# Low part of every second half of a weight tile: an accumulating DMA onto a negated high part in place of a VectorE subtraction

## The chip, the cores and the metric

The kernel runs on one core of one Trainium2 chip. The metric is the device time of one execution in microseconds (us); lower is better. All durations below come from one profiled execution of the kernel before, unless they are called times of runs.

## The reference, cut to what matters

The reference is one decoder block on 256 tokens of width 2048, in float32: an RMS norm, an input projection, two mixers side by side (gated linear attention with four heads, and a gated short convolution), a merge of the two, an output projection with a residual, a second norm, an MLP with a hidden width of 8192, and a last norm.

```python
proj = jnp.einsum('bsd,dn->bsn', h, w_in[l])          # q, k, v, r, lr, cb, cc, cx, ga, gb
...
y_a = jnp.einsum('bse,ed->bsd', o * jax.nn.silu(r), w_gla_out[l])
u = causal_depthwise_conv(cc * cx, conv_w[l])
y_b = jnp.einsum('bsc,cd->bsd', cb * u, w_conv_out[l])
merged = jax.nn.sigmoid(ga) * y_a + jax.nn.sigmoid(gb) * y_b
x = x + jnp.einsum('bsd,de->bse', merged, w_o[l])
hid = jnp.square(jax.nn.relu(jnp.einsum('bsd,df->bsf', h2, w_ffn_up[l])))
x = x + jnp.einsum('bsf,fd->bsd', hid, w_ffn_down[l])
```

Nearly all of the work is matrix products of 256 tokens with large weights: about 300 weight tiles of 1 MB, each read from HBM once.

## The kernel before, in words

**Split products.** Every float32 operand of a large product is split into a high part, rounded to the format float32r, and a low part, the rest. A product is then the sum of three float32r passes: high by high, high by low, low by high. Activations lie in the resident tiles A and B, whose 512 columns hold 256 columns of the high part and 256 of the low part.

**A weight tile.** `wsplit` (L44 to L55) loads one tile of 128 partitions by 2048 columns (1 MB) with a DMA of the SyncE queue into one of 4 buffers `wst` (L45, L46). It then works on two halves of 1024 columns. For each half ScalarE writes the high part `whi` by a rounding copy (L52), and VectorE subtracts it from the loaded half to give the low part `wlo` (L53). `whi` and `wlo` have 5 buffers each, that is two and a half tiles.

**Stationary tiles.** `ws_product` (L57) takes a tile as 16 blocks of 128 columns that are loaded into TensorE as weights. For each block it multiplies `whi` with 512 columns of the activation (L67) and `wlo` with 256 (L69, and L66 for the last block). 221 tiles go this way: the last five of q, those of k, of the convolution branch, of the gates, of the three output projections and of the MLP's up-projection. The first eight blocks use the first half of a tile, the last eight the second. Each product is then gathered by a ScalarE copy (`corr`, L75) and a VectorE addition (L76).

**Moving tiles.** `xs_product` (L408) streams a tile as the moving operand, 24 matmuls of 512 columns per tile (L420 to L422), half of them with the first half of the tile. 78 tiles go this way: those of v and of the MLP's down-projection but two (these two are split at L596 and L597 into the place of B).

**The start.** The first three tiles of q are loaded in quarters into `wst` buffers of their own (L139), split at L165 and L166 while they land, and multiplied at L174 to L176. They take three of the four `wst` buffers. After them TensorE does the small product of the gate's rank-16 input (L185), a sum (L198), and then the first tile that comes by way of `wsplit`.

**Order of the work.** Each engine runs its own list of instructions in order, and waits at each for the buffers and operands that it needs. The list is made when the program is built. A tile's load waits until its `wst` buffer has been read by all four split instructions of the tile that had it before; a split instruction waits until TensorE has finished with the buffer that it overwrites. PSUM holds four product banks (`mmp`).

Of the kernel before, what the change touches and what calls it, by code (L numbers as in the profile page):

```python
# [7 lines left out]
F32 = mybir.dt.float32  # L8
F32R = mybir.dt.float32r
U8 = mybir.dt.uint8  # L10
AF = mybir.ActivationFunctionType
ALU = mybir.AluOpType
PSUM = bass.MemoryType.PSUM

P = 128
T = 256          # tokens
D = 2048
KT = D // P      # contraction tiles of a D-wide product
EPS = 1e-6
# [3 lines left out]
NM = len(LEVELS) * 64 + 128 + 3 * 64  # L23
NQ = 4           # the hidden layer is walked in quarters


@with_exitstack
def block_kernel(ctx, tc, xT, wq, wk, wlr, wv, wr, wcb, wcc, wcx, wga, wgb, wgu,
                 wgla, wconv, wo, wup, wdown, cols, gfin, consts, masks, out):
    """Activations lie transposed ([feature, token]); every float32 operand of a large product is  # L30
    split exactly into two float32r parts and the product is summed from three float32r passes."""
    nc = tc.nc

    cpool = ctx.enter_context(tc.tile_pool(name="cpool", bufs=1))
    apool = ctx.enter_context(tc.tile_pool(name="apool", bufs=1))
    wst = ctx.enter_context(tc.tile_pool(name="wst", bufs=4))
    wsp = ctx.enter_context(tc.tile_pool(name="wsp", bufs=5))
# [4 lines left out]

# [1 line left out]
    def wsplit(src):  # L44
        st = wst.tile([P, 2048], F32, tag="wst", name="wst_t")  # L45
        nc.sync.dma_start(out=st, in_=src)  # L46
        halves = []
        for hf in range(2):
            s = st[:, hf * 1024:(hf + 1) * 1024]
            hi = wsp.tile([P, 1024], F32R, tag="whi", name="whi")  # L50
            lo = wsp.tile([P, 1024], F32R, tag="wlo", name="wlo")
            nc.scalar.copy(out=hi, in_=s)  # L52
            nc.vector.tensor_sub(out=lo, in0=s, in1=hi.bitcast(F32))  # L53
            halves.append((hi, lo))
        return halves  # L55

    def ws_product(src, act):  # L57
        """[128 features, 256 tokens] as (main, correction) in one PSUM bank."""
        halves = wsplit(src)
        ps = mmp.tile([P, 512], F32, tag="mm", name="ps_mm")  # L60
        for kt in range(KT):
            hi, lo = halves[kt // 8]
            sl = slice((kt % 8) * P, (kt % 8 + 1) * P)
            last = kt == KT - 1
            if last:
                nc.tensor.matmul(ps[:, T:], lhsT=lo[:, sl], rhs=act[kt][:, :T], start=False, stop=False)  # L66
            nc.tensor.matmul(ps, lhsT=hi[:, sl], rhs=act[kt], start=(kt == 0), stop=last)  # L67
            if not last:
                nc.tensor.matmul(ps[:, T:], lhsT=lo[:, sl], rhs=act[kt][:, :T], start=False, stop=False)  # L69
        return ps[:, :T], ps[:, T:]  # L70

# [14 lines left out]
    def rsqrt_mean(ms, shape, tag, bufs=1):  # L86
        """1/sqrt(ms) with one Newton step; ms is kept."""
        y = tp.tile(shape, F32, tag=tag, name=tag, bufs=bufs)
        t = tp.tile(shape, F32, tag=tag + "_t", name=tag + "_t", bufs=bufs)
        nc.scalar.activation(t, ms, AF.Sqrt)  # L90
        nc.vector.reciprocal(out=y, in_=t)
        nc.vector.tensor_mul(out=t, in0=y, in1=y)
        nc.vector.scalar_tensor_tensor(out=t, in0=t, scalar=-0.5, in1=ms, op0=ALU.mult, op1=ALU.mult)
        nc.vector.scalar_tensor_tensor(out=y, in0=t, scalar=1.5, in1=y, op0=ALU.add, op1=ALU.mult)
        return y

# [1 line left out]
    A = [apool.tile([P, 512], F32R, tag=f"A{i}", name=f"A{i}") for i in range(KT)]  # L98
# [34 lines left out]

# [1 line left out]
    NF = 3  # L135
    with tc.tile_pool(name="xpool", bufs=1) as xpool:
# [6 lines left out]
        for g in range(4):  # L143
# [14 lines left out]
            for j in range(NF):  # L158
                if g % 2 == 0:
                    fsp[j] = (wsp.tile([P, 1024], F32R, tag="whi", name="whi"),  # L160
                              wsp.tile([P, 1024], F32R, tag="wlo", name="wlo"))
                hi, lo = fsp[j]
                q4 = slice((g % 2) * 512, (g % 2 + 1) * 512)
                ws = fst[j][:, g * 512:(g + 1) * 512]
                nc.scalar.copy(out=hi[:, q4], in_=ws)  # L165
                nc.vector.tensor_sub(out=lo[:, q4], in0=ws, in1=hi[:, q4].bitcast(F32))  # L166
                ps = fps[j]
                for i in range(4):
                    kt = g * 4 + i
                    sl = slice((kt % 8) * P, (kt % 8 + 1) * P)  # L170
                    last = kt == KT - 1
                    if last:
                        nc.tensor.matmul(ps[:, T:], lhsT=lo[:, sl], rhs=A[kt][:, :T], start=False, stop=False)
                    nc.tensor.matmul(ps, lhsT=hi[:, sl], rhs=A[kt], start=(kt == 0), stop=last)  # L174
                    if not last:
                        nc.tensor.matmul(ps[:, T:], lhsT=lo[:, sl], rhs=A[kt][:, :T], start=False, stop=False)  # L176
        nc.sync.dma_start(out=wl_st, in_=wlr)
        nc.sync.dma_start(out=cst, in_=consts)

        # columns 0-15 are the high parts, 32-47 the low ones; the gate product adds their rows  # L180
        nc.scalar.copy(out=wl, in_=wl_st)
# [5 lines left out]
        st = stp.tile([P, T], F32, tag="st", name="st_x")  # L187
        acc = cum[:, 0:2, :]  # cum is not in use yet
        for g in range(8):
# [20 lines left out]

# [1 line left out]
    with tc.tile_pool(name="p2a", bufs=1) as p2a:  # L212
# [5 lines left out]
        def gate(jj):  # L218
            """cum of four tiles: 16 times the log gates, then their sums within each token tile."""
            pgs, abs_ = [], []  # L220
# [37 lines left out]

# [1 line left out]
    def score_level(hd, li):  # L260
# [35 lines left out]
    def score_rest(hd):  # L296
        """The pairs of neighbours: s = t, the levels of one and two tokens; and the keys of the first
        token tile for the queries of the second. Few pairs per query: their products are summed over
        the features by a product with ones, which leaves each sum on every row."""
        hs = slice(2 * hd, 2 * hd + 2)  # L300
# [64 lines left out]
    def next_unit():  # L365
        """The products of the unit prepared a step ago, then the next unit's operands."""
        if ready:
# [8 lines left out]

# [1 line left out]
    pz = [cpool.tile([P, T + 2], F32, name=f"pz{i}") for i in range(2)]  # L378
# [23 lines left out]

# [1 line left out]
    p3 = ExitStack()  # L404
# [3 lines left out]
    def xs_product(srcs, act):  # L408
        """Two PSUM banks [128 tokens, 512] of act^T W."""
        pss = [mmp.tile([P, 512], F32, tag="mm", name="ps_xs") for _ in range(2)]  # L410
# [19 lines left out]

# [1 line left out]
    tb = vp.tile([P, KT, T], F32, name="tb")  # L432
# [43 lines left out]

# [1 line left out]
    o, ssum = o0  # L478
# [18 lines left out]

# [1 line left out]
    sga = vp.tile([P, KT, T], F32, tag="v", name="sga")  # L499
# [9 lines left out]

# [1 line left out]
    mp = ctx.enter_context(tc.tile_pool(name="mp", bufs=1))  # L511
# [27 lines left out]

# [1 line left out]
    ssq = cpool.tile([P, 2, 5], F32, name="ssq")  # L541
# [3 lines left out]
    def down_evac(ps, m, c0, w, k):  # L545
        """Adds a product to the residual; its sum of squares goes to column k of the last norm's."""
        xs = xtok[:, m, c0:c0 + w]
# [36 lines left out]

    # The last chunk's weights stay whole on chip (half of them where the operand B was), so that the
    # first token tile is finished and stored under the products of the second one.
    wres = []
# [30 lines left out]
def _stationary(np, w):  # L618
    """[K, N] -> [N/128, K/2048, 128 (k), 16 (k tile), 128 (n)], one contiguous megabyte per tile."""
    k, n = w.shape  # L620
    return np.ascontiguousarray(
        w.reshape(k // 2048, 16, 128, n // 128, 128).transpose(3, 0, 2, 1, 4)).reshape(-1, 128, 2048)


def _moving(np, w):
    """[K, N] -> [K/2048, N/512, 4, 128 (k), 4 (k tile), 512 (n)], one contiguous megabyte per tile."""
    k, n = w.shape
# [62 lines left out]
```

## Time and profile before

| what | value |
|---|---|
| time of runs before, median of 2 | 1765.72 us (1765.39 to 1766.05) |
| span of the profiled execution, first to last instruction | 1764.1 us |
| what lies outside the span (median less span) | 1.6 us |
| mean granted TensorE clock | 0.999 |
| data read from HBM over the span | 325.17 MB |

The profile gives, for each engine, how long it was busy, what it waited for, and when each instruction ran. PE is TensorE's matmuls, PEld its weight loads, DVE is VectorE, ACT is ScalarE, POOL is GpSimd, SP is SyncE; a q behind the name means the engine's DMA queue. "DMA share" is the mean busy share of the core's 16 DMA engines. A wait is written "who <- whom".

### The profile page before, as it was taken

What the parts mean: (1) busy time and instruction counts of PE and PEld (TensorE: products, weight loads), DVE (VectorE), ACT (ScalarE), POOL (GpSimd) and SP (SyncE); (2) the same over time, 40 slices, a digit from 0 to 9 for tenths busy, and PEclk for the clock granted to TensorE, in tenths of its full rate; (3) what the DMA queues carried; (4) which work ended last, traced back from release to release, by engine and by line L of the source; (5) the groups of instructions that cost most, each with busy time, mean ns of one, the idle gap of its engine ahead of it and who ended that gap; (6) DMA issues with size and microseconds to landing.
All of it is one profiled execution on the core that took longest, in us unless ns stands there. A gap on an engine that the chain in (4) does not pass through costs nothing.

```text
span 1764.1 us, 23853 instructions
## 1 busy us (share of the span) xinstructions
PE 1749.0 (99%) x9468; PEld 1502.3 (85%) x9468; DVE 1161.8 (66%) x1717; ACT 856.3 (49%) x1178; POOL 0.2 (0%) x4
## 2 busy tenths in 40 slices
PE   8999999999999999999999999999999999999998
PEld 6888888888888888888888888888888888888887
DVE  8978888765555558875676666655665566556664
ACT  7745454444344446654544454434443354334451
POOL 0000000000000000000000000000000000000000
PEclk9999999999999999999999999999999999999999
DMA  8454444555555544455555555555555555555552
GB/s 312 169 192 167 167 170 167 177 181 193 196 184 188 191 177 160 166 199 189 191 183 208 213 191 183 187 193 193 188 191 191 191 191 190 192 191 191 181 190 83
DMA packets 50158, 328.81 MB, mean 186 GB/s; under 512 B 5694, under 2 KB 7870, under 8 KB 11391
## 3 DMA queue, kind: packets, MB, share of 16 engines
q1 hardware_dynamic: 47376, 323.55, 51.5%
q10 hardware_dynamic: 2670, 3.74, 0.6%
q8 instruction: 74, 1.21, 0.3%
q14 instruction: 38, 0.30, 0.0%
HBM read 325.17 MB, written 2.10 MB: 186 GB/s over the span
## 4 chain that ended last, share of the span: by engine, by line
PE 99%; DMA 0%; DVE 0%; ACT 0%; SPq 0%; issue 0%; DVEq 0%; ACTq 0%
PE ps_mm L67 47%; PE ps_mm L69 22%; PE ps_xs L421 8%; PE ps_xs L422 8%; PE ps_xs L420 8%; PE ps_mm L66 1%; PE sp L286 1%; PE ps_mm L174 1%; PE ps_xs L612 0%; PE ps_xs L611 0%; PE ps_xs L610 0%; PE po L446 0%; PE ps_mm L176 0%; DMA wst_t<-in_wq 0%; PE ps_lr L185 0%; PE po L448 0%
## 5 line engine op out<-in xcount | busy, mean ns | idle before, releaser
L53 DVE TENSOR_TENSOR wlo<-wst_t,whi 128x1024 fp32r<-128x1024 f32 x598 | 731.5, 1224 | 374.4 <-ACT whi L52 366.1
L52 ACT CAST whi<-wst_t 128x1024 fp32r<-128x1024 f32 x598 | 628.7, 1052 | 483.1 <-PE ps_mm L67 242.0
L67 PE MATMUL ps_mm<-A,whi 128*128 128x512 f32 x2000 | 707.5, 399 | 0.0
L67 PE MATMUL ps_mm<-B,whi 128*128 128x512 f32 x1536 | 538.7, 399 | 0.0
L69 PE MATMUL ps_mm<-A,wlo 128*128 128x256 f32 x1875 | 527.1, 281 | 0.0
L67 PEld LDWEIGHTS ps_mm<-A,whi 128*128 128x128 f32 x2000 | 370.9, 188 | 79.1
L69 PE MATMUL ps_mm<-B,wlo 128*128 128x256 f32 x1440 | 404.5, 281 | 0.0
L69 PEld LDWEIGHTS ps_mm<-A,wlo 128*128 128x128 f32 x1875 | 354.0, 189 | 4.1
L67 PEld LDWEIGHTS ps_mm<-B,whi 128*128 128x128 f32 x1536 | 283.6, 188 | 62.5
L69 PEld LDWEIGHTS ps_mm<-B,wlo 128*128 128x128 f32 x1440 | 271.9, 189 | 4.6
L75 ACT COPY corr<-ps_mm 128x256 f32<-128x256 f32 x208 | 77.3, 372 | 347.0 <-PE ps_mm L67 346.2
L420 PE MATMUL ps_xs<-whi,A 128*128 128x512 f32 x608 | 236.5, 389 | 0.0
L421 PE MATMUL ps_xs<-wlo,A 128*128 128x512 f32 x608 | 236.5, 389 | 0.0
L422 PE MATMUL ps_xs<-whi,A 128*128 128x512 f32 x608 | 236.5, 389 | 0.0
L76 DVE TENSOR_TENSOR t<-ps_mm,corr 128x256 f32<-128x256 f32 x208 | 88.1, 424 | 176.3 <-ACT corr L75 176.1
L421 PEld LDWEIGHTS ps_xs<-wlo,A 128*128 128x128 f32 x608 | 114.1, 188 | 23.8
L420 PEld LDWEIGHTS ps_xs<-whi,A 128*128 128x128 f32 x608 | 114.1, 188 | 23.7
L422 PEld LDWEIGHTS ps_xs<-whi,A 128*128 128x128 f32 x608 | 114.1, 188 | 23.4
L83 ACT CAST A<-t 128x256 fp32r<-128x256 f32 x80 | 32.6, 408 | 7.6 <-DVE t L506 7.4
L66 PE MATMUL ps_mm<-A,wlo 128*128 128x256 f32 x125 | 35.2, 282 | 0.0
L84 DVE TENSOR_TENSOR A<-t,A 128x256 fp32r<-128x256 f32 x80 | 33.5, 419 | 0.0
L548 DVE SCALAR_TENSOR_TENSOR xtok<-ps_xs,rs,xtok 128x512 f32<-128x512 f32 (+1 forms) x33 | 22.8, 728 | 14.5 <-PE ps_xs L612 14.5
(171 smaller groups left out, 798.3 us busy)
## 6 DMA issues: line engine op xcount, KB each, us to landing
wst_t<-in_wup SPq DMA_DIRECT2D x64, 1024.0 KB, 4.8
wst_t<-in_wdown SPq DMA_DIRECT2D x64, 1024.0 KB, 4.8
wst_t<-in_wcc SPq DMA_DIRECT2D x16, 1024.0 KB, 4.8
wst_t<-in_wcx SPq DMA_DIRECT2D x16, 1024.0 KB, 4.8
wst_t<-in_wcb SPq DMA_DIRECT2D x16, 1024.0 KB, 4.8
wst_t<-in_wv SPq DMA_DIRECT2D x16, 1024.0 KB, 4.8
wst_t<-in_wgb SPq DMA_DIRECT2D x16, 1024.0 KB, 4.7
wst_t<-in_wconv SPq DMA_DIRECT2D x16, 1024.0 KB, 4.8
```

The lines of the kernel that those rows point to most:

```text
L52: nc.scalar.copy(out=hi, in_=s)
L53: nc.vector.tensor_sub(out=lo, in0=s, in1=hi.bitcast(F32))
L66: nc.tensor.matmul(ps[:, T:], lhsT=lo[:, sl], rhs=act[kt][:, :T], start=False, stop=False)
L67: nc.tensor.matmul(ps, lhsT=hi[:, sl], rhs=act[kt], start=(kt == 0), stop=last)
L69: nc.tensor.matmul(ps[:, T:], lhsT=lo[:, sl], rhs=act[kt][:, :T], start=False, stop=False)
L75: nc.scalar.copy(out=c, in_=corr)
L76: nc.vector.tensor_add(out=out_t, in0=main, in1=c)
L83: nc.scalar.copy(out=dst[:, :T], in_=src)
L84: nc.vector.tensor_sub(out=dst[:, T:], in0=src, in1=dst[:, :T].bitcast(F32))
L420: nc.tensor.matmul(pss[m], lhsT=ah, rhs=hi[:, sl], start=(kt == 0), stop=False)
L421: nc.tensor.matmul(pss[m], lhsT=ah, rhs=lo[:, sl], start=False, stop=False)
L422: nc.tensor.matmul(pss[m], lhsT=al, rhs=hi[:, sl], start=False, stop=(kt == len(srcs) * 4 - 1))
```

## The change

`wsplit` treats the two halves of a tile differently. The first half is as before. For the second half ScalarE first writes the negated half, rounded, into a tile `wla` (an activation with scale -1), then the high part as before; and a DMA issued by GpSimd adds the same half tile, read a second time from HBM, onto `wla`. Its 1024 columns by 128 partitions are 0.5 MB. VectorE does nothing for the second half. To make room, `wst` goes from 4 buffers to 3 and `wlo` from 5 to 3 (now first halves alone, so three tiles), and `wla` has 4 (four tiles). `whi` keeps its 5. The first three tiles of q still use VectorE alone, with the 3 `wlo` buffers. The rest of the difference is comments.

```diff
-    wst = ctx.enter_context(tc.tile_pool(name="wst", bufs=4))
+    wst = ctx.enter_context(tc.tile_pool(name="wst", bufs=3))
     wsp = ctx.enter_context(tc.tile_pool(name="wsp", bufs=5))
...
     def wsplit(src):
         st = wst.tile([P, 2048], F32, tag="wst", name="wst_t")
         nc.sync.dma_start(out=st, in_=src)
         halves = []
         for hf in range(2):
             s = st[:, hf * 1024:(hf + 1) * 1024]
             hi = wsp.tile([P, 1024], F32R, tag="whi", name="whi")
-            lo = wsp.tile([P, 1024], F32R, tag="wlo", name="wlo")
-            nc.scalar.copy(out=hi, in_=s)
-            nc.vector.tensor_sub(out=lo, in0=s, in1=hi.bitcast(F32))
+            if hf == 0:
+                lo = wsp.tile([P, 1024], F32R, tag="wlo", name="wlo", bufs=3)
+                nc.scalar.copy(out=hi, in_=s)
+                nc.vector.tensor_sub(out=lo, in0=s, in1=hi.bitcast(F32))
+            else:
+                lo = wsp.tile([P, 1024], F32R, tag="wla", name="wla", bufs=4)
+                nc.scalar.activation(lo, s, AF.Copy, scale=-1.0)
+                nc.scalar.copy(out=hi, in_=s)
+                nc.gpsimd.dma_start(out=lo, in_=src[:, 1024:], accum_op=ALU.add)
             halves.append((hi, lo))
         return halves
...
                     fsp[j] = (wsp.tile([P, 1024], F32R, tag="whi", name="whi"),
-                              wsp.tile([P, 1024], F32R, tag="wlo", name="wlo"))
+                              wsp.tile([P, 1024], F32R, tag="wlo", name="wlo", bufs=3))
```

Two places show how the lists of instructions stand. The first is ScalarE's list in the MLP's up-projection, where the numbers behind the names tell the tiles apart: a tile's load is `wst_t_N`, and the next tile's number is higher by 51 or 52. Before, for two products:

```order
L75 COPY corr_9983<-ps_mm_9949 128x256
L52 CAST whi_10094<-wst_t_10092 128x1024
L83 CAST A5_84<-t1_9986 128x256
L52 CAST whi_10098<-wst_t_10092 128x1024
L75 COPY corr_10034<-ps_mm_10000 128x256
L52 CAST whi_10145<-wst_t_10143 128x1024
L83 CAST A6_85<-t1_10037 128x256
L52 CAST whi_10149<-wst_t_10143 128x1024
```

And of the changed kernel, at the same place:

```order
L83 COPY corr_10110<-ps_mm_10076 128x256
L55 CAST whi_10223<-wst_t_10221 128x1024
L91 CAST A4_83<-t1_10113 128x256
L60 CAST whi_10227<-wst_t_10221 128x1024
L59 ACTIVATE wla_10332<-wst_t_10325 128x1024
L83 COPY corr_10162<-ps_mm_10128 128x256
L55 CAST whi_10275<-wst_t_10273 128x1024
L91 CAST A5_84<-t1_10165 128x256
L60 CAST whi_10279<-wst_t_10273 128x1024
L59 ACTIVATE wla_10384<-wst_t_10377 128x1024
```

Between the second high part of a tile (L60) and the gathering of a product (L83 COPY) there now stands the negation (L59) of a tile two further on: 10325 beside 10221.

The second place is GpSimd's list, which before held four fills of constants and nothing of the program's own. Its beginning now, where `wla` is the tile that the DMA adds onto and the name behind the arrow is the weight in HBM:

```order
L690 MEMSET const-uint8-127 128x1
L694 UNCONDITIONAL_BRANCH
L61 DMA wla<-in_wq 128x1024 x5
L61 DMA wla<-in_wk 128x1024 x8
L61 DMA wla<-in_wcc 128x1024
L61 DMA wla<-in_wcx 128x1024
L61 DMA wla<-in_wcb 128x1024
```

There are 299 such DMAs, one for each tile that goes through `wsplit`, in the order of the tiles.

## Rows read from the trace of the kernel before

**Rows 1.** The page, part 1: busy time, share of the span and instructions per engine.

```profile
PE 1749.0 (99%) x9468; PEld 1502.3 (85%) x9468; DVE 1161.8 (66%) x1717; ACT 856.3 (49%) x1178; POOL 0.2 (0%) x4
```

**Rows 2.** The page, part 4: the chain that ended last, shares of the span.

```profile
PE 99%; DMA 0%; DVE 0%; ACT 0%; SPq 0%; issue 0%; DVEq 0%; ACTq 0%
```

**Rows 3.** Timeline of ACT in the up-projection: start, us, engine, line, work [idle <-releaser].

```profile
1064.65 1.05 ACT L52 CAST whi<-wst_t 128x1024 fp32r<-128x1024 f32 x1 [0.97 <-PE ps_mm L67]
1067.61 0.37 ACT L75 COPY corr<-ps_mm 128x256 f32<-128x256 f32 x1 [1.90 <-PE ps_mm L67]
1067.87 1.05 ACT L52 CAST whi<-wst_t 128x1024 fp32r<-128x1024 f32 x1
1068.93 0.41 ACT L83 CAST A<-t 128x256 fp32r<-128x256 f32 x1
1070.30 1.05 ACT L52 CAST whi<-wst_t 128x1024 fp32r<-128x1024 f32 x1 [0.97 <-PE ps_mm L67]
```

**Rows 4.** Timeline of ACT in the down-projection.

```profile
1200.67 1.06 ACT L52 CAST whi<-wst_t 128x1024 fp32r<-128x1024 f32 x1 [1.67 <-PE ps_xs L422]
1203.39 1.05 ACT L52 CAST whi<-wst_t 128x1024 fp32r<-128x1024 f32 x1 [1.66 <-PE ps_xs L422]
1206.12 1.05 ACT L52 CAST whi<-wst_t 128x1024 fp32r<-128x1024 f32 x1 [1.67 <-PE ps_xs L422]
```

**Rows 5.** Groups by line and shape: count, busy us, mean ns, idle before.

```profile
L53 DVE TENSOR_TENSOR wlo<-wst_t,whi 128x1024 fp32r<-128x1024 f32 x598 | 731.5, 1224 | 374.4 <-ACT whi L52 366.1
...
L83 ACT CAST A<-t 128x256 fp32r<-128x256 f32 x80 | 32.6, 408 | 7.6 <-DVE t L506 7.4
...
L270 ACT ACTIVATE e<-e 128x512 f32<-128x512 f32 x20 | 12.6, 629 | 6.5 <-DVE e L268 6.5
...
L155 ACT ACTIVATE A<-xt,colt 128x256 fp32r<-128x256 f32 x16 | 6.9, 498 | 2.4 <-DMA xt<-in_xT 2.4
...
L165 ACT CAST whi<-wst_t 128x512 fp32r<-128x512 f32 x12 | 6.8, 613 | 1.5 <-DMA wst_t<-in_wq 1.5
```

**Rows 6.** Stretches: PE, PEld, DVE, ACT, POOL busy (count), PEclk, DMA share, GB/s.

```profile
40.00:65.00 25.00, 25.00 (x141) 21.80 (x140) 20.89 (x45) 23.32 (x32) 0.00 (x0) 1.00 0.47 170
65.00:90.00 25.00, 25.00 (x144) 21.72 (x143) 25.00 (x50) 13.51 (x21) 0.00 (x0) 1.00 0.52 189
...
10.00:20.00 10.00, 10.00 (x52) 8.45 (x52) 9.88 (x20) 9.72 (x22) 0.00 (x0) 1.00 1.05 403
```

**Rows 7.** DMA from 1200 to 1222 us: queue, packets, MB, share; issues, us to landing.

```profile
q1 hardware_dynamic: 576, 4.19, 54.8%
...
wst_t<-in_wup SPq DMA_DIRECT2D x4, 1024.0 KB, 4.9
```

**Rows 8.** DMA from 30 to 36 us, where the queues of SP (q1) and ACT (q10) overlap.

```profile
q1 hardware_dynamic: 240, 1.74, 74.4%
q10 hardware_dynamic: 113, 0.35, 22.6%
...
wst_t<-in_wk SPq DMA_DIRECT2D x1, 1024.0 KB, 5.3
```

**Rows 9.** DMA from 10 to 20 us, issues: count, KB each, us to landing.

```profile
wst_t<-in_wq SPq DMA_DIRECT2D x1, 1024.0 KB, 7.8
```

**Rows 10.** Timeline of the start: SP's queue, VectorE, TensorE.

```profile
15.31 14.24 SPq L46 DMA_DIRECT2D wst_t<-in_wq  x5
...
21.70 1.90 DVE L166 TENSOR_TENSOR wlo<-wst_t,whi 128x512 fp32r<-128x512 f32 x3
...
30.22 0.58 PE L67 MATMUL ps_mm<-A,whi 128*128 128x512 f32 x1
```

## The prediction, made before the changed kernel ran

> **What bounds the kernel now.** I read the busy times first. TensorE's matmuls cover 1749.0 of the 1764.1 us; VectorE is busy for 66% and ScalarE for 49% [rows 1]. Busy shares alone could deceive, so the chain that ended last came next: 99% of it is TensorE [rows 2]. The 15 us that TensorE is idle lie before its first matmul and behind its last. So what the change takes away, VectorE's work, stands nowhere on the path. Then I looked at what the others wait for, in a timeline of ScalarE: before each rounding copy L52 it sits idle for 0.97 to 1.90 us, released by TensorE [rows 3, 4]. The splitting runs ahead as far as its buffers let it and is held back by TensorE, not the other way round.
>
> The same timelines give the pace. The same copy comes back after 1070.30 - 1064.65 = 5.65 us, the time of a stationary tile [rows 3]; two halves of a moving tile take 1206.12 - 1200.67 = 5.45 us [rows 4]. These are the budgets that every other engine, the DMA engines among them, has to meet. I therefore look for a load that comes to more than 5.45 or 5.65 us per tile.
>
> **VectorE.** 299 subtractions of 1.224 us go [rows 5]: 366 us, which leaves 796 (45%). On the path: 0, as nothing waits for VectorE. Even from 65 to 90 us, where it is busy for 25.00 of 25 us, TensorE is too [rows 6].
>
> **ScalarE.** 299 negations come. The nearest rows: an ACTIVATE is slower than a CAST of the same shape by 16 ns at 512 columns (629 against 613) and by 90 at 256 (498 against 408) [rows 5]; a CAST of 1024 columns takes 1.05 us [rows 3]. So 1.07 to 1.14 us each, I take 1.1: 329 us more, 1185 in all (67%). Per tile of the up-projection: 2 x 1.05 + 0.37 + 0.41 + 1.1 = 4.0 of 5.65 us. Its cover is thus the idle time of ScalarE before L52. It is gone in one place: from 40 to 65 us, with the gates' functions, ScalarE is busy for 23.32 of 25 us [rows 6], and 25 / 5.65 = 4.4 negations add 4.9. That is 3.2 us too many. The split is up to two and a half tiles ahead, some 14 us, and from 65 to 90 us ScalarE has 25 - 13.51 - 4.9 = 6.6 us to catch up. Cost between 0 and 3.2; I take 1.
>
> **The added wait.** ScalarE's negation stands two tiles ahead of the high parts, as the list shows, and waits for that tile's load and for TensorE to end the tile that had its `wla` buffer four tiles before. Behind it stand the gathering copy and the next high parts. Numbering the tile that TensorE has just ended as 1, the negation is that of tile 5 and the next high part that of tile 4. The latter is needed only two tiles later, 11 us, and the sum of `wla` three and a half tiles later, some 19 us. A landing of 4.9 us [rows 7] or 7.8 behind others [rows 9] is hidden by either. With 3 `wst` buffers the load of tile 5 starts when the second high part of tile 2 is done, in the middle of tile 0, and has one and a half tiles, 8.2 us or more, less the copy's 1.05 us. It takes 4.9. What is late next, if transfers get slower, is this load (second rival).
>
> **DMA.** This decides. A full load now takes 54.8% of 22 us for 4.19 MB, or four tiles: 3.0 us of the 16 engines per tile [rows 7]. But these are single transfers with a rise and a fall. Where transfers are queued behind each other the engines moved 403 GB/s at a share of 1.05 [rows 6], so 1.05 MB costs 2.60 us when nothing is left idle. Two queues share the engines: from 30 to 36 us theirs take 74.4% and 22.6% [rows 8], so the shares add up, and a load landed after 5.3 us in place of 4.9.
>
> The accumulating DMA is in no row; nothing in the trace comes from GpSimd's queue. Bounds: its 0.5 MB pass the engines at least once, 1.3 us at the full rate. At most each byte passes three times one after the other, read from HBM, read from SBUF, written: 3.9 us (at the price of single transfers, 4.5). I take 2.6 us, as the nearest row is that of a plain 1 MB load: the accumulation has just as much to read, 0.5 MB from HBM and 0.5 MB of what it adds onto, and a plain copy's writing does not show as a time of its own. Sum per tile: 2.6 + 2.6 = 5.2 us, 92% of 5.65 and 95% of 5.45. It fits, by little. Cost: 0, from 0 to (6.5 - 5.65) x 221 + (6.5 - 5.45) x 78 = 188 + 82 = 270 us.
>
> A rule bears on this. The Trainium skill (Collectives: The Full Stack, The bandwidth ceiling) has it that an add inside the DMA costs nothing of itself, but needs two source reads on the same ring, and gives 62.28 against 32.35 GB/s for a copy and a reduction, a ratio of 1.93. By that the 0.5 MB would be an estimated 1.3 x 1.93 = 2.5 us and the sum 5.1, which fits too; by three passes it would be 6.5, which does not. No run here shows yet which holds.
>
> **GpSimd.** It has 0.2 us of work [rows 1] and now one issue per tile. SyncE's issues are one per tile as well and are never on the chain. I take 0; it would cost only if an issue took more than 5.45 us.
>
> **The start.** Three `wst` buffers are all taken by the first three tiles of q. Before, the fourth tile's load was issued at 15.31 us [rows 10] and landed 7.8 us later [rows 9]. Now it waits for the last subtraction of the first tile, 21.70 us + a third of 1.90, so it is issued at 22.4 and lands after 4.9 to 7.8 us, at 27.3 to 30.2. High part 1.05 and subtraction 1.22: its first half is ready at 29.6 to 32.5, where TensorE wanted it at 30.22 [rows 10]. Its second half: negation until 29.5 to 32.4, then an issue and a landing again like a load's, 34.4 to 40.2, where TensorE wants it at 30.2 + 2.8 = 33.0. So 1.4 to 7 us late; I take 3, nearer to the lower end, as a half tile has half the bytes.
>
> **Sum.** 1764.1 + 1.6 outside the span = 1765.7, which is the median of the runs; + 3 start + 1 gates + 0 = 1770 us. From below: TensorE has no wait to give back, so nothing in the rows can bring more than a few us.
>
> **First rival: the DMA engines become the bound.** It decides as soon as load plus accumulation take over 5.45 (moving) or 5.65 us (stationary), that is from 2.85 or 3.05 us for the accumulation, only 10 to 17% above my value. It costs the excess in every tile. If both transfers cost as in single transfers, 3.0 + 3.0 = 6.0: 0.35 x 221 + 0.55 x 78 = 120 us, so 1886 us. If each byte passes three times, 1765.7 + 270 = 2036 us. For it: the margin of 5 to 8%, the 3.0 us that a load in fact shows, and smaller pieces (rows of 4 KB for 8 KB). Against: the 403 GB/s.
>
> **Second rival: ScalarE held up by a late load.** Load of tile 5, negation of 5, gathering, high parts of 4, which free the buffer for the load of 7: a loop over two tiles. If the load lands after 2.6 + 2.6 + the 2.3 us that 4.9 has beyond its 2.6, because an accumulation always runs beside it, it is 7.5 + 0.3 issue + 1.1 + 0.37 + 0.41 + 2.1 = 11.8 us against 2 x 5.65 = 11.3. That is 0.25 per tile, 55 us over 221: 1821 us. Against it: the accumulation of an earlier tile is issued by the negation that precedes the load's last stretch, so the two overlap only in part.
>
> **Third rival: faster.** TensorE would have to run faster without VectorE's second stream of reads; for 2%, 35 us, a tile would have to take 5.53 in place of 5.65 us: 1730 us. No row supports it: beside a VectorE that is full from 65 to 90 us TensorE is busy throughout at a clock of 1.00 [rows 6].
>
> **How the numbers follow.** Forecast 53%; first rival 34%, second 11%, third 2%. A measurement of this kernel tells about 2% from no change. Both slower rivals lie beyond 1801, so slower has 45%, same 53%, faster 2%. The forecast's own range is 1763 to 1790. For 8 in 10 the range must take in most of the first rival: 1762 to 2036, its three-pass end; what is left out is mainly an accumulation dearer than that.
>
> **What would show it.** Right: a new queue with 157 MB, landing within 10 us; DMA share near 0.9; TensorE still 98% busy; the only new TensorE wait near 30 us. Wrong: TensorE waiting for `wla` in every tile, at L67 or L69 in mid tile, with the DMA share at its ceiling (first rival), or ScalarE's L59 waiting for the load of `wst_t` (second). A tile time above 5.65 us in the up-projection gives the accumulation's price at once.

## The result, and the profile after

The changed kernel takes 1846.18 us (two runs, 1845.93 to 1846.43) against 1765.72 us before: 1.0456 times as long, 95% interval 1.0436 to 1.0475. That is 80.5 us slower. The prediction's likeliest case, 1770 us and no change, did not come; the time lies in the range of 1762 to 2036, and on the side of the slower rivals.

The page of the changed kernel, parts 1, 3 and 4, answers to [rows 1] and [rows 2]:

```profile
PE 1774.9 (96%) x9468; PEld 1503.9 (82%) x9468; DVE 805.3 (44%) x1418; ACT 1111.7 (60%) x1479; POOL 258.4 (14%) x303
...
q0 software_dynamic: 43056, 156.78, 48.7%
q1 hardware_dynamic: 47376, 323.55, 45.9%
...
DMA 45%; PE 26%; ACT 11%; issue 10%; DVE 6%; POOL 0%; ACTq 0%; SPq 0%; DVEq 0%; POOLq 0%
```

VectorE lost the work that it was to lose, 1161.8 to 805.3 us. TensorE's idle time went from 15 to 70 us, and its busy time from 1749 to 1775. A lower clock after stops is a part of these 26 us: the mean granted clock was 0.993 against 0.999, an estimated 0.006 x 1845 = 11 us. But some 15 of the 26 lie in the MLP (633.0 against 618.4 us busy from its first up-projection load to the last), at a mean granted clock of 1.00; that the profile counts short waits of matmuls there as busy time is likely, but not shown. The chain, 99% TensorE before, now runs through DMA for 45%. A quick reading of this page of the profile says: the DMA engines are 95% busy, so they are full. The experiments show that this reading is wrong.

The list of waits of the changed kernel (who <- whom, us in total, times, longest) points elsewhere. Before, none of its long rows had ScalarE waiting for a load:

```profile
ACT wla L59 <- DMA wst_t<-in_wdown: 151.2, 59, 5.3
ACT wla L59 <- DMA wst_t<-in_wup: 151.0, 58, 6.1
...
PE ps_mm L77 <- DVE wlo L56: 15.6, 25, 1.3
...
PE ps_mm L77 <- DMA wla<-in_wq: 8.4, 3, 7.3
```

The negation L59 waits for loads for hundreds of us; this is the sign that the prediction named for its second rival. TensorE waits longest in all for `wlo`, the low part of a *first* half, which no accumulation makes. It is late because its high part stands behind the negation of another tile in ScalarE's list. Only at the start does TensorE wait for an accumulation worth naming.

The timeline of ScalarE, 1250 to 1270 us, shows it (start, us, work, and the idle time before with its releaser); compare [rows 3, 4]:

```profile
1250.50 1.06 ACT L59 ACTIVATE wla<-wst_t 128x1024 fp32r<-128x1024 f32 x1 [1.12 <-DMA wst_t<-in_wdown]
1251.46 1.03 ACT L55 CAST whi<-wst_t 128x1024 fp32r<-128x1024 f32 x1
1252.40 1.05 ACT L60 CAST whi<-wst_t 128x1024 fp32r<-128x1024 f32 x1
1258.58 1.06 ACT L59 ACTIVATE wla<-wst_t 128x1024 fp32r<-128x1024 f32 x1 [5.13 <-DMA wst_t<-in_wup]
1259.54 1.03 ACT L55 CAST whi<-wst_t 128x1024 fp32r<-128x1024 f32 x1
1260.48 1.04 ACT L60 CAST whi<-wst_t 128x1024 fp32r<-128x1024 f32 x1
```

Before, it was TensorE that released the copies. Now ScalarE stands for 5.13 us at a negation whose load has not landed, and then at once does the two high parts of another tile, whose load had landed long before.

The issues of the MLP's loads in the changed kernel, with microseconds to landing (counted from the start of the issue, median), and the time of the first and the last of the 64 up-projection loads. Before, they landed after 4.8:

```profile
wst_t<-in_wup SPq DMA_DIRECT2D x64, 1024.0 KB, 8.0
...
wla<-in_wup POOLq DMA_DIRECT2D x64, 512.0 KB, 8.0
...
L48 SPq DMA_DIRECT2D wst_t<-in_wup x64: 327/328/328, 1060.4 to 1713.7; - x64
```

From the first to the last of them are 111 tiles (63 stationary, 48 moving). They take 653.3 us, 5.89 each; before, the same row ran from 1015.0 to 1633.4, 618.4 us, 5.57 each. So 35 of the 80 us are lost here. This stretch is the yardstick below ("the MLP stretch").

### The profile page after: what moved, and what is told of

Same layout as the page of the kernel before. It is cut to its first block, busy times and chain, and to the rows that moved or that the text cites. A ratio compares the mean times of both kernels' runs of the same rounds, so it can differ in the third digit from the quotient of the medians.

```text
span 1844.6 us, 24535 instructions
## 1 busy us (share of the span) xinstructions
PE 1774.9 (96%) x9468; PEld 1503.9 (82%) x9468; DVE 805.3 (44%) x1418; ACT 1111.7 (60%) x1479; POOL 258.4 (14%) x303
## 3 DMA queue, kind: packets, MB, share of 16 engines
q0 software_dynamic: 43056, 156.78, 48.7%
## 4 chain that ended last, share of the span: by engine, by line
DMA 45%; PE 26%; ACT 11%; issue 10%; DVE 6%; POOL 0%; ACTq 0%; SPq 0%; DVEq 0%; POOLq 0%
PE ps_mm L75 15%; DMA wst_t<-in_wup 12%; DMA wst_t<-in_wdown 11%; PE ps_mm L77 7%; DMA wst_t<-in_wconv 6%; ACT whi L55 5%; DVE wlo L56 4%; DMA wst_t<-in_wga 3%; DMA wst_t<-in_wgla 3%; ACT whi L60 3%; DMA wst_t<-in_wr 3%; DMA wst_t<-in_wv 2%; DMA wst_t<-in_wo 2%; ACT corr L83 1%; ACT wla L59 1%
## 5 line engine op out<-in xcount | busy, mean ns | idle before, releaser
L59 ACT ACTIVATE wla<-wst_t 128x1024 fp32r<-128x1024 f32 x299 | 317.0, 1060 | 623.2 <-DMA wst_t<-in_wdown 151.2
L56 DVE TENSOR_TENSOR wlo<-wst_t,whi 128x1024 fp32r<-128x1024 f32 x299 | 365.8, 1223 | 356.9 <-ACT whi L55 348.9
L60 ACT CAST whi<-wst_t 128x1024 fp32r<-128x1024 f32 x299 | 312.4, 1045 | 10.3 <-PE ps_mm L75 10.3
L77 PE MATMUL ps_mm<-A,wlo 128*128 128x256 f32 x1000 | 283.5, 284 | 6.1 <-DVE wlo L56 6.0
L77 PE MATMUL ps_mm<-A,wla 128*128 128x256 f32 x875 | 247.0, 282 | 8.4 <-DMA wla<-in_wq 8.4
L77 PE MATMUL ps_mm<-B,wlo 128*128 128x256 f32 x768 | 218.5, 285 | 9.8 <-DVE wlo L56 9.6
L77 PEld LDWEIGHTS ps_mm<-A,wlo 128*128 128x128 f32 x1000 | 189.7, 190 | 13.9 <-DVE wlo L56 10.2
L77 PE MATMUL ps_mm<-B,wla 128*128 128x256 f32 x672 | 189.1, 281 | 0.9 <-DMA wla<-in_wup 0.9
L77 PEld LDWEIGHTS ps_mm<-A,wla 128*128 128x128 f32 x875 | 166.4, 190 | 9.4 <-DMA wla<-in_wq 9.4
L77 PEld LDWEIGHTS ps_mm<-B,wlo 128*128 128x128 f32 x768 | 145.8, 190 | 21.8 <-DVE wlo L56 18.1
L429 PE MATMUL ps_xs<-wlo,A 128*128 128x512 f32 x304 | 121.5, 400 | 10.9 <-DVE wlo L56 10.7
L77 PEld LDWEIGHTS ps_mm<-B,wla 128*128 128x128 f32 x672 | 127.2, 189 | 1.3 <-DMA wla<-in_wup 1.3
```

The costliest lines, as they stand in the source:

```text
L59: nc.scalar.activation(lo, s, AF.Copy, scale=-1.0)
L429: nc.tensor.matmul(pss[m], lhsT=ah, rhs=lo[:, sl], start=False, stop=False)
```

## The experiments

Two theories stood against each other. A: the DMA engines are full, a load and an accumulation together take about 5.8 us, more than a tile. B: the engines have room, but ScalarE's list holds up the high parts behind a negation that waits for a load. The loop is: load of tile n, negation of n, the two high parts of n-1, which free the staging buffer (`wst`) for the load of n+2.

**The transfers by themselves.** A kernel of transfers alone, in seven phases:

```diff
+    for i in range(N):                       # accumulating, float32r
+        nc.gpsimd.dma_start(out=d[i % R], in_=w[i, :, 1024:], accum_op=ALU.add)
...
+    for i in range(N):                       # loads of 1 MB beside accumulating ones
+        nc.sync.dma_start(out=fl[i % 3], in_=w[24 + i])
+        nc.gpsimd.dma_start(out=f[i % R], in_=w[i, :, 1024:], accum_op=ALU.add)
```

> Transfers alone, no block computed: seven phases of 24 transfers of 0.5 MB each, four in flight (plain from SyncE; plain from GpSimd; accumulating in float32; accumulating in float32r; accumulating with the source in SBUF; then 24 loads of 1 MB beside 24 accumulations; 24 loads beside 24 plain ones). Theory A (the DMA engines are full, an accumulation costs about twice a plain transfer or more): plain 1.3 us each, accumulating 2.6 to 3.0 us each, a load beside an accumulation together 5.4 to 5.9 us. Theory B (the engines have room, ScalarE's list holds the loads up): accumulating 1.3 to 2.3 us each, load and accumulation together under 5.2 us. If the rounding to float32r costs something, the float32r phase is longer than the float32 one.

The timeline of GpSimd's issues (start, us an issue, and the wait before): plain (`b`), accumulating in float32 (`c`), in float32r (`d`), from SBUF (`e`), beside loads of 1 MB (`f`):

```profile
53.83 0.53 POOL L43 DMA_DIRECT2D b<-in_wup  x1 [0.72 <-DMA b<-in_wup]
55.12 0.53 POOL L43 DMA_DIRECT2D b<-in_wup  x1 [0.76 <-DMA b<-in_wup]
...
101.11 0.86 POOL L47 DMA_DIRECT2D c<-in_wup  x1 [1.66 <-DMA c<-in_wup]
103.58 0.86 POOL L47 DMA_DIRECT2D c<-in_wup  x1 [1.60 <-DMA c<-in_wup]
...
150.85 0.86 POOL L51 DMA_DIRECT2D d<-in_wup  x1 [1.66 <-DMA d<-in_wup]
153.32 0.86 POOL L51 DMA_DIRECT2D d<-in_wup  x1 [1.60 <-DMA d<-in_wup]
...
215.49 0.86 POOL L55 DMA_DIRECT2D e<-a  x1 [1.62 <-DMA e<-a]
217.97 0.85 POOL L55 DMA_DIRECT2D e<-a  x1 [1.62 <-DMA e<-a]
...
318.22 0.86 POOL L62 DMA_DIRECT2D f<-in_wup  x1 [4.16 <-DMA f<-in_wup]
323.22 0.86 POOL L62 DMA_DIRECT2D f<-in_wup  x1 [4.14 <-DMA f<-in_wup]
328.25 0.86 POOL L62 DMA_DIRECT2D f<-in_wup  x1 [4.16 <-DMA f<-in_wup]
```

With four transfers in flight each issue follows a landing, so the distance of two rows is the price: 2.48 us accumulating (217.97 - 215.49), the same in float32, in float32r and from SBUF. Plain, it is 1.3 us where the issues follow each other evenly, as in the two rows; that phase has gaps, with which its mean is 316 GB/s, or 1.66 us a transfer. A pair of a load and an accumulation takes 5.02 us (10.03 over two). That is the capacity: below 5.45 and 5.65. Theory A's price per pair is wrong; the price that theory B gave an accumulation (1.3 to 2.3 us) was a little low.

**Without the accumulation.**

```diff
-                nc.gpsimd.dma_start(out=lo, in_=src[:, 1024:], accum_op=ALU.add)
+                nc.gpsimd.dma_start(out=lo, in_=src[:, 1024:])
```

> The changed kernel with the accumulation left out of the DMA, which copies the half tile plainly; the sum of the low part is therefore left out. Same bytes from HBM, same lists. Theory A: an engine time of about 2.8 + 1.4 = 4.2 us per tile, the waits at L59 vanish but for the start: 1765 to 1785 us. Theory B (the second stream delays the loads, whatever it costs the engines): still 1810 to 1846 us.

1778.06 us, 1.0062 times before (1.0039 to 1.0085). This row speaks for A as it was written down, as plain transfers cost the engines half. It doesn't tell the theories apart after all: loads land after 6.8 us in it, not 8.0, which also takes the loop of theory B off the path (worked out below). The MLP stretch took 618.8 us.

**A fourth staging buffer, and the negation one tile nearer.**

```diff
-    wst = ctx.enter_context(tc.tile_pool(name="wst", bufs=3))
+    wst = ctx.enter_context(tc.tile_pool(name="wst", bufs=4))
...
-                lo = wsp.tile([P, 1024], F32R, tag="wlo", name="wlo", bufs=3)
+                lo = wsp.tile([P, 1024], F32R, tag="wlo", name="wlo", bufs=2)
...
-                lo = wsp.tile([P, 1024], F32R, tag="wla", name="wla", bufs=4)
+                lo = wsp.tile([P, 1024], F32R, tag="wla", name="wla", bufs=3)
...
```

> Four wst buffers again, paid for by one wla (3) and one wlo (2); nothing is left out. The negation is then one tile nearer to its use and its load one tile earlier. Theory A: the tile time stays that of the engines, about 5.8 us; only the start improves: 1820 to 1846 us. Theory B: the loop over load, negation and high part is broken: 1765 to 1785 us.

1778.71 us, 1.0067 (1.0045 to 1.009), with every accumulation in place. Of its page of the profile, part 3, then the list of waits:

```profile
q0 software_dynamic: 43056, 156.78, 49.6%
q1 hardware_dynamic: 47376, 323.55, 47.1%
...
ACT wla L59 <- PE ps_mm L74: 303.0, 201, 1.7
```

The same bytes in the same two queues, at a share of 97%, and in the MLP TensorE is no longer held up: the negation now waits for TensorE. The MLP stretch took 618.3 us (1025.4 to 1643.7), as long as before. Theory A can't stand beside this.

**No negation.** The accumulations go onto four fixed tiles.

```diff
-                lo = wsp.tile([P, 1024], F32R, tag="wla", name="wla", bufs=4)
-                nc.scalar.activation(lo, s, AF.Copy, scale=-1.0)
+                lo = wla4[turn[0] % 4]
+                turn[0] += 1
...
```

> The negation is left out: the DMA accumulates onto four fixed tiles that are zeroed once, so the low parts of second halves are wrong sums. The DMA traffic is that of the changed kernel, ScalarE never waits for a load two tiles ahead. Theory A: the traffic sets the pace: 1825 to 1850 us. Theory B: 1765 to 1785 us.

1781.17 us, 1.008 (1.0051 to 1.0109). With the traffic kept, and the instruction that waits for the load two tiles on taken out of ScalarE's list, the time comes back, though staging has its 3 buffers.

**One number.** The run with four staging buffers changed two things, the staging and the place of the negation; they had to be told apart.

```diff
-                lo = wsp.tile([P, 1024], F32R, tag="wla", name="wla", bufs=4)
+                lo = wsp.tile([P, 1024], F32R, tag="wla", name="wla", bufs=3)
```

> The changed kernel with one number changed: wla has 3 buffers, not 4. The list then has the negation one tile further on instead of two ahead of the next high part; DMA traffic, staging buffers and instruction counts stay. Theory B (ScalarE held up by the load that the negation waits for): the waits of L59 on loads vanish, the tile time returns to 5.65 and 5.45 us, what is left is the start: 1775 to 1785 us. Theory A (engines full at 5.8 us per tile): 1840 to 1850 us. Theory C (the three staging buffers are what is short): still above 1820 us, as loads start no earlier.

1784.08 us, 1.0097 (1.0082 to 1.0112): 62 of the 80 us are back with a buffer *less*. The number of `wla` buffers decides where the negation stands. In the list of the up-projection the negation behind the second high part of a tile is that of the tile two further on with 4 buffers, of the next tile with 3, and of the tile itself with 2. With 3:

```order
L60 CAST whi_10227<-wst_t_10221 128x1024
L59 ACTIVATE wla_10280<-wst_t_10273 128x1024
L83 COPY corr_10162<-ps_mm_10128 128x256
L55 CAST whi_10275<-wst_t_10273 128x1024
```

The negation is that of the very next tile, 10273, whose high part comes two instructions later. ScalarE's timeline, then the row of the whole MLP stretch of this kernel (PE, PEld, DVE, ACT, POOL busy, PEclk, DMA share, GB/s):

```profile
1255.84 1.06 ACT L59 ACTIVATE wla<-wst_t 128x1024 fp32r<-128x1024 f32 x1 [1.61 <-PE ps_mm L74]
1256.80 0.35 ACT L83 COPY corr<-ps_mm 128x256 f32<-128x256 f32 x1
1257.05 1.05 ACT L55 CAST whi<-wst_t 128x1024 fp32r<-128x1024 f32 x1
1258.10 0.41 ACT L91 CAST A<-t 128x256 fp32r<-128x256 f32 x1
1258.83 1.05 ACT L60 CAST whi<-wst_t 128x1024 fp32r<-128x1024 f32 x1 [0.32 <-PE ps_mm L75]
1261.49 1.06 ACT L59 ACTIVATE wla<-wst_t 128x1024 fp32r<-128x1024 f32 x1 [1.61 <-PE ps_mm L74]
...
1069.00:1723.00 654.00, 654.00 (x3329) 555.42 (x3329) 240.45 (x339) 405.62 (x488) 101.97 (x118) 1.00 1.00 284
```

The period is 1261.49 - 1255.84 = 5.65 us again and TensorE has no gap in the stretch. The same stretch of the changed kernel:

```profile
1069.00:1723.00 654.00, 633.73 (x3197) 527.59 (x3196) 226.34 (x324) 372.92 (x463) 95.83 (x111) 1.00 0.97 268
```

With a *higher* DMA share, 1.00 against 0.97, the faster kernel moves 284 against 268 GB/s. Theory C fell too: 3 staging buffers are enough.

**Two buffers for the sums.** The same number, one further down.

```diff
-                lo = wsp.tile([P, 1024], F32R, tag="wla", name="wla", bufs=4)
+                lo = wsp.tile([P, 1024], F32R, tag="wla", name="wla", bufs=2)
```

> The changed kernel with 2 wla buffers. The negation then never waits for a load, but it can run only when TensorE has ended the tile two before: 1.06 us for it, 0.9 for the issue and 7.7 for the landing are 9.7 us, where TensorE gets to the second half after one and a half tiles, 8.5 us. Theory B with this lead time: TensorE waits for wla, some 1.2 us in every tile or, if the waits fall on every second one, half of that: 1850 to 2000 us, and the waits are named wla, not L59 on a load. If only the place of the negation before loads mattered: 1775 to 1790 us, as with 3 buffers.

2189.46 us, 1.24 (1.2275 to 1.2523), far more than expected, with the waits on `wla` that were expected. Of its list of waits:

```profile
PEld ps_xs L429 <- DMA wla<-in_wdown: 103.4, 52, 6.0
...
PE ps_mm L77 <- DMA wla<-in_wup: 71.8, 49, 4.9
```

The mistake was to count the lateness once. It closes on itself: the negation of tile n waits for TensorE to end tile n-2, then come 1.06 us for it, 0.3 until the issue starts, a landing of 10.1 here (the issue is part of it), and half a tile of TensorE, 2.8: 14.3 us for two tiles, 7.1 each. The MLP stretch shows 799.6 / 111 = 7.2. So of the three numbers tried the middle one is best: at 4 the negation meets loads that have not landed, at 2 the sums come too late.

**The start.** Buffers alone, on the kernel before, every low part by VectorE:

```diff
-    wst = ctx.enter_context(tc.tile_pool(name="wst", bufs=4))
+    wst = ctx.enter_context(tc.tile_pool(name="wst", bufs=3))
...
-            lo = wsp.tile([P, 1024], F32R, tag="wlo", name="wlo")
+            lo = wsp.tile([P, 1024], F32R, tag="wlo", name="wlo", bufs=4)
```

> The kernel before with 3 wst buffers and 4 wlo, nothing else: every low part by VectorE, no GpSimd DMA. If the start's loss of some 12 us comes from the fourth tile's load having to wait for a buffer: 1768 to 1775 us. If it comes from the accumulations: 1765 to 1768 us.

1768.85 us, 1.0016 (1.0007 to 1.0026): 3.2 us. And the changed kernel with accumulations from the 14th split tile on:

```diff
+                if turn[0] <= 13:
+                    nc.scalar.copy(out=hi, in_=s)
+                    nc.vector.tensor_sub(out=lo, in0=s, in1=hi.bitcast(F32))
+                else:
```

> The changed kernel, but the 13 tiles of q and k that go through the split get their second low part from VectorE as before (in a wla buffer); accumulations start with the convolution's tiles. If the start and the gates lose 12 to 17 us through ScalarE's and GpSimd's added work there: 1830 to 1838 us; if the buffers alone are the reason, less than 5 us come back: 1841 to 1846 us.

1828.23 us, 18.0 less than the changed kernel, a little more than the 8 to 16 that the first case allowed; the median is below its 1830. In the MLP it is as slow as the changed kernel (654.4 us). So the start and the gates cost about 18 us, some 3 of them for the buffers if the two runs may be added up so, and 18 + 62 make up the 80.

**Both mended.**

```diff
-    wst = ctx.enter_context(tc.tile_pool(name="wst", bufs=3))
+    wst = ctx.enter_context(tc.tile_pool(name="wst", bufs=4))
...
+                lo = wsp.tile([P, 1024], F32R, tag="wlo", name="wlo", bufs=2)
...
+                lo = wsp.tile([P, 1024], F32R, tag="wla", name="wla", bufs=3)
+                if turn[0] <= 13:
...
```

> Four wst, three wla, two wlo buffers, and accumulations only from the convolution's tiles on; nothing left out. Theory B with a start as before: 1765 to 1769 us, no faster than before, as TensorE sets the pace throughout.

1770.24 us, 1.0023 (1.0014 to 1.0033), 1 us over what was expected. With 286 accumulating DMAs, and 286 of the 598 subtractions gone from VectorE, the kernel is within 5 us of where it was (what these 5 us are was not tried), and no run of the block came below the kernel before: there was nothing on the path to take away.

## Where the prediction was right and where wrong, step by step

The forecast itself, 1770 us and no change, with a chance of 53%, did not come. That the range held 1846 us is luck: its upper end, 2036, was set for DMA engines through which every byte passes three times, and that did not happen.

**Right: the bound of the kernel before.** TensorE sets the pace, nothing waits for VectorE, and its 357 us brought nothing. The run "Both mended" shows it: 1770 us with nearly all of that work gone. (The 1.90 us of [rows 3] stands before a gathering copy, not before a rounding copy, and one of the copies there has no wait; nothing hangs on it.)

**Right: the sum of the DMA engines.** Taken were 2.6 us for an accumulation and 5.2 for the pair; measured were 2.48 and 5.02. So the first rival, given 34%, was not what happened, though the 95% of the profile looks like it. Nor does the tile time of 5.89 us give "the accumulation's price at once", as the prediction's last sentence has it. The rule of the Trainium skill (Collectives: The Full Stack, The bandwidth ceiling), two source reads and an add for nothing, is stated for rings between cores, with a ratio of 1.93. The trace agrees where plain transfers follow each other evenly: 2.48 us against 1.29 (55.12 - 53.83) is 1.92; by the means of the two phases, 316 GB/s plain and 210 accumulating, it is 1.5.

**Right: ScalarE's and GpSimd's prices.** 1.06 us a negation (1.1 taken), and an issue of 0.86 us, far from 5.45.

**Wrong: the step "The added wait", and with it the case against the second rival.** There the load was said to have 8.2 us less 1.05, to take 4.9, and to be hidden, and the load's lengthening was dismissed since load and accumulation overlap "only in part". The loop that the second rival names was the right one; the landing time was the mistake. Loads land after 8.0 us, later than even the 8.2 - 1.05 = 7.1 of that step. One turn of the loop in the changed kernel: the issue of a load, ScalarE's part, and the issue of the load two further on; then the issue behind the negation at 1258.58, shown above, in the down-projection:

```profile
1465.21 0.33 SPq L48 DMA_DIRECT2D wst_t<-in_wup  x1
...
1473.26 1.06 ACT L59 ACTIVATE wla<-wst_t 128x1024 fp32r<-128x1024 f32 x1 [1.21 <-DMA wst_t<-in_wup]
1474.23 0.35 ACT L83 COPY corr<-ps_mm 128x256 f32<-128x256 f32 x1
1474.48 1.05 ACT L55 CAST whi<-wst_t 128x1024 fp32r<-128x1024 f32 x1
1475.53 0.41 ACT L91 CAST A<-t 128x256 fp32r<-128x256 f32 x1
1475.85 1.04 ACT L60 CAST whi<-wst_t 128x1024 fp32r<-128x1024 f32 x1
...
1476.92 0.33 SPq L48 DMA_DIRECT2D wst_t<-in_wup  x1
...
1261.89 0.33 SPq L48 DMA_DIRECT2D wst_t<-in_wup  x1
```

From the start of the issue to the negation pass 8.05 us, the landing and 0.1; from there to the next issue 3.66. That is 11.7 us for two stationary tiles, where TensorE needs 11.3. For two moving tiles the second part is 1261.89 - 1258.58 = 3.3, and 8.1 + 3.3 = 11.4 us stand against 10.9. Over 63 and 48 tiles that is 5.85 x 63 + 5.7 x 48 = 642 us; with 8.2, the mean of the landings in place of the median, it is 655. Measured were 653.3. The same sum says from what landing time the loop decides: 11.3 - 3.8 = 7.5 and 10.9 - 3.4 = 7.5 us. With plain second reads the loads landed after 6.8, and nothing was lost. With four staging buffers and with three `wla` buffers, where the negation stands elsewhere, they landed after 7.3 to 7.6 us beside the same traffic. So 8.0 is not the traffic's alone; what adds the rest in the changed kernel was not tried.

The rival's form in the prediction gave 55 us, with 7.5 us for a load and nothing for moving tiles; 62 were measured for the place of the negation. That the two are close is luck: its sum counts the issue of 0.3 us a second time, and by the loop as the trace shows it, 7.5 us for a load is just the time from which it begins to decide. The prediction had numbered the buffers rightly, and then compared each with its deadline one by one. The deadline of 11 us for the next high part holds when nothing else stands behind the negation; but each late negation also makes the next load late.

**Wrong in size: the start.** Taken were 3 us and 1 for the gates, against some 18. The prediction gave 1.4 to 7 us for the first sum and took 3. TensorE asked for it at 32.7 and had it at 40.0, at the far end. Its DMA was issued at 29.35, as early as the prediction had it, but landed 10.6 us later in place of 4.9 to 7.8, beside two loads, a second accumulation and two other transfers; that half a tile has half the bytes was no reason for the lower end. The timeline of its issue, then the DMA rows from 24 to 42 us:

```profile
29.35 1.01 POOL L61 DMA_DIRECT2D wla<-in_wq  x1 [28.90 <-ACT wla L59]
...
wst_t<-in_wq SPq DMA_DIRECT2D x2, 1024.0 KB, 9.1
wla<-in_wq POOLq DMA_DIRECT2D x2, 512.0 KB, 10.6
```

What the stop costs beyond itself is in the clock (stretches of the changed kernel, PEclk the third number from the end):

```profile
36.00:40.00 4.00, 0.00 (x0) 0.00 (x0) 0.00 (x0) 0.00 (x0) 0.00 (x0) 0.64 1.04 283
40.00:42.00 2.00, 1.99 (x6) 1.80 (x7) 0.92 (x3) 0.00 (x0) 0.00 (x0) 0.50 1.05 315
42.00:44.00 2.00, 2.00 (x8) 1.65 (x7) 1.95 (x6) 0.00 (x0) 0.00 (x0) 0.52 0.70 246
44.00:47.00 3.00, 3.00 (x19) 2.63 (x18) 1.37 (x2) 2.30 (x4) 0.00 (x0) 1.00 0.02 4
```

TensorE stands for 7.3 us, in which its granted clock falls, is then granted 0.50 to 0.52, the lower of its two levels (1.2 GHz), for 4 us, and manages 14 recorded matmuls in them against 19 in the next 3 us. How the rest of the 18 us is shared between this and ScalarE's load at the gates was not tried.

## What to carry to other kernels

Ask of every instruction that a scheduler moves ahead what it waits for, and what stands behind it on its engine; where a wait on a transfer closes a loop through a buffer, add the loop up once around, with the landing time that the transfer has beside the new traffic, and don't compare its parts with their deadlines one by one. A buffer more can be worse than one less, when the number of buffers decides how far ahead an instruction is put. And relief of an engine that nobody waits for buys nothing.

## What was not expected of the hardware

- A DMA share near 1 doesn't show full engines here, where two queues run beside each other. The changed kernel moved 268 GB/s at 0.97 in the MLP, the one with 3 `wla` buffers 284 at 1.00, the transfers alone 314 with both queues at 52%. By this count the packets of one accumulation take 48.7% of 1844.6 us / 299 = 3.0 us of engine time, where it costs 2.48 alone; that the time of a packet includes some waiting is the likely reason, not shown by itself.
- An accumulation costs the same 2.48 us whether its source lies in HBM or in SBUF, and whether its target is float32 or float32r. Its issue takes GpSimd 0.86 us, a plain one 0.53.
